# A 128-token product inside a Strassen-ordered MLP: three split products or one plain float32 product

## The chip, the cores and the metric

The kernel runs on one core of a Trainium2 chip. The metric is the device time of one execution in microseconds; the time before is the median of three runs.

## The reference, cut to what matters

One layer of a hybrid backbone is computed for one context sequence of 128 tokens and one latent sequence of 2048 tokens. The change concerns the MLP at the end of the layer, and in it the context tokens alone:

```python
h = rmsnorm(x, norm_ffn_l) * (1.0 + sc2) + sh2
x = x + ga2 * (jnp.square(jax.nn.relu(h @ w_ff1_l)) @ w_ff2_l)
```

D_MODEL is 1024 and D_FF is 4096, all in float32. `h @ w_ff1` of the 128 context tokens is a product of 128x1024 by 1024x4096. The same product of the 2048 latent tokens is sixteen times as large.

## The kernel before, in words

**Tokens.** There are 17 tiles of 128 tokens: tile 0 is the context, tiles 1 to 16 are the latent tokens. The mixer's stages come first; the MLP follows and fills the second half of the span. The first MLP product is the stage in question.

**Split products.** TensorE multiplies `float32r` operands in one product. To keep accuracy, a float32 operand is split by `split4` into a high part (a cast on ScalarE, `wH`) and the remainder (a subtraction on VectorE, `wL`). `mm3` (lines 225 to 227) then issues three products for each 128-deep slice: high x high, high x low, low x high.

**Units.** `w_ff1` is cut into 16 pieces of 256 columns. The latent tokens are two groups of eight tiles, `g` = 0 and 1, so there are 32 units: `n` = 0 to 15 for group 0, 16 to 31 for group 1. In a unit the 2x2 blocks of the weights (column half `i`, contraction half `kh`: the tiles `raw[i, kh]`) are multiplied with the tokens by a Strassen-Winograd scheme of seven products, numbered 1 to 7 and run in `ORDER` = 1, 5, 6, 7, 3, 2, 4. Each product is 4 slices x 3 split products of 512 tokens. The tokens' side lies ready in the tiles `hop[g, o]`, loaded from HBM (`hop_next`, two DMAs of 1 MB each); the weights' side is made in `Unit.weights(o)` from the `raw` tiles, which `Unit.loads` fetches.

**The context tile.** Its 128 tokens do not fit the scheme, so the units of group 1 do it beside the seven products: `Unit.single` multiplies the four blocks of `raw` with the two halves of `x0` (the context tile's activations), and sums them in one PSUM bank, `ps0`, of a block (two units in the first and last block of the group, one unit in the others). Before, `single` uses the split weights that products 1, 2 and 4 need anyway, and one split more (`w[0]`, of `raw[1, 0]`, made for this alone as "product" 0). `x0` is split once by `first_tile`. `single_out` squares the ReLU of the bank and stores it to `z_d[0]`.

**What sets the order.** `seq` lists all (product, unit) pairs. The loop over positions `p` calls, in this order, the loads of position p + LEAD + 8 (14 ahead), the weights of position p + LEAD (6 ahead), the context tile's and the norm's side steps, and the product of position p. Loads and stores all go through SP's DMA queue. The engines' streams are then ordered by a list scheduler that pulls instructions forward when its own plan sees their inputs ready, so that the streams are not simply the order of the code. Tiles named `w` (raw, split and result tiles alike, 49 of 2 KB a partition) share one pool, and the eight PSUM banks named `f` another: a new tile waits until an old one is released.

**The last positions.** From position `last` = len(seq) - 16 on, the loop also prepares the second MLP product (`s_next`, `t_next`: casts and subtractions of `zraw` and `traw`, into `zH`, `zL` and the tokens' tiles).

Of the kernel before, what the change touches and what calls it, by code (L numbers as in the profile page):

```python
# [17 lines left out]
P = 128  # L18
# [34 lines left out]
NV = 7  # L53
LEAD = 6
ORDER = (1, 5, 6, 7, 3, 2, 4)
NK = DFF // P // 2
AHEAD = 3
WINDOWS = [2.46, 0.03, -0.51, 1.06, -1.61, 18.16, 17.58, 18.3,
# [4 lines left out]
def hybrid_step(  # L63
# [7 lines left out]
    V, A, G, T = nc.vector, nc.scalar, nc.gpsimd, nc.tensor  # L71
# [12 lines left out]
    def f32(ap):  # L84
        return ap.bitcast(F32)
# [25 lines left out]
    hop_d = {(g, o): dp.tile([P, 4, 2, 4, P], F32, name=f"hop_{g}_{o}_d") for g in range(2) for o in range(1, 8)}  # L111
    z_d = [dp.tile([4 if a else 1, P, 2, NK, P], F32, name=f"z{a}_d") for a in range(5)]
    s1_d, s2_d = ([dp.tile([4, P, NK, P], F32, name=f"s{i}{g}_d") for g in range(2)] for i in (1, 2))
    t_d = {(i, k): dp.tile([P, 512], F32, name=f"t{i}_{k}_d") for i in (5, 6, 7, 4) for k in range(NK)}

# [96 lines left out]
    def w512(name, dt=F32):  # L212
        return wp.tile([P, 512], dt, tag="w", name=name)
# [7 lines left out]
    def mm3(ps, trip, first=True, last=True, more=False):  # L221

        n = len(trip)
        for i, (lh, ll, rh, rl) in enumerate(trip):
            T.matmul(ps, lh, rh, start=first and i == 0, stop=False, skip_group_check=more)  # L225
            T.matmul(ps, lh, rl, start=False, stop=False, skip_group_check=more)  # L226
            T.matmul(ps, ll, rh, start=False, stop=last and i == n - 1, skip_group_check=more)  # L227
# [47 lines left out]
    with ExitStack() as ph:  # L275
# [8 lines left out]
        def pt():  # L284
            return ppt.tile([P, 512], F32, tag="pt", name="pt", bufs=3)
# [7 lines left out]
        for d in range(2):  # L293
            m = p1.tile([P, P], F32, tag=f"mcum{d}", name=f"mcum{d}", bufs=1)
# [102 lines left out]
        ps = pt()  # L397
# [378 lines left out]
        for bi in range(len(BLOCKS)):  # L776
            nxt = prep_block(bi + 1) if bi + 1 < len(BLOCKS) else None
            if bi == 0:
                order = [(1, 0), (1, 1), (1, 2), (0, 0), (0, 1), (1, 3), (0, 2), (0, 3)]
            else:  # L780
                order = [(gi, h) for gi in (1, 0) for h in range(4)]
            order = order + [(2, h) for h in range(4)]
            at = {e: n for n, e in enumerate(order)}
            tile_of = {}
            for n, (gi, h) in enumerate(order):
                u = us[n] if bi == 0 and n < 3 else feature_tile(blk, bi, gi, h)
# [141 lines left out]
    hops = {}  # L928
    hop_order = [(g, o) for g in range(2) for o in ORDER]
    hop = {}  # L930

    def hop_tile(dt, n):

        side, bufs = ("A", 2) if n else ("B", 5)
        return hops[side].tile([P, 4, 2, 4, P], dt, tag="hop", name="hop", bufs=bufs)

    def hop_next():
        g, o = hop_order.pop(0)
        hop[g, o] = t = hop_tile(F32R, o in ORDER[:2])
        for k in range(0, 4, 2):  # L940
            load(out=f32(t)[:, k : k + 2], in_=hop_d[g, o][:, k : k + 2])


    with ExitStack() as ph:
# [234 lines left out]
        units = [unit(t, 0) for t in range(NT)] + [unit(t, 1) for t in [0] + list(range(NT - 1, 0, -1))]  # L1179
# [205 lines left out]
        for i, u in enumerate(units):  # L1385
            w = p2 if i <= NT else p3
            at(i - 3 if i > PL else -10, u["prep_loads"])
            at(i - 1, u["scan_loads"])
            n = len(u["prep"])
# [5 lines left out]
            if i >= NT:  # L1395
                at(i, lambda u=u: o_loads(u))
                first, second = o_steps(u)
# [66 lines left out]
    def bank():  # L1464
        return psq.tile([P, 512], F32, tag="f", name="f", bufs=8)

    def add(out, a, b, op=ALU.add):
        V.tensor_tensor(out=out, in0=a, in1=b, op=op)  # L1468

    def split4(src, name="w"):  # L1470

        h = wp.tile([P, 4, P], F32R, tag="w", name=name + "H")
        lo = wp.tile([P, 4, P], F32R, tag="w", name=name + "L")
        A.copy(h, src)  # L1474
        add(lo, src, f32(h), ALU.subtract)
        return h, lo

    def as4(t):
        return t.rearrange("p (a d) -> p a d", a=4)


    NP = DFF // 256
    x0 = []

    class Unit:
# [14 lines left out]
        def weights(self, o):  # L1500

            a, w, t = self.raw, self.w, self.t
            if o == 1:
                w[1] = split4(a[0, 0])
            elif o == 5:
                t["s"] = as4(w512("s"))
                add(t["s"], a[1, 0], a[1, 1])
                w[5] = split4(t["s"])
            elif o == 6:
                add(t["s"], t["s"], a[0, 0], ALU.subtract)  # L1510
                w[6] = split4(t["s"])
            elif o == 7:
                d = as4(w512("d"))
                add(d, a[0, 0], a[1, 0], ALU.subtract)
                w[7] = split4(d)
            elif o == 3:
                add(t["s"], a[0, 1], t["s"], ALU.subtract)
                w[3] = split4(t["s"])
            elif o == 2:
                w[2] = split4(a[0, 1])  # L1520
            elif o == 0:
                w[0] = split4(a[1, 0])
            else:
                w[4] = split4(a[1, 1])

# [58 lines left out]

        def single(self, o, ps, i, first, last):

            if o not in (1, 2, 0, 4):
                return
            c = (2 * i + (o in (0, 4))) * P
            k0 = 4 * (o in (2, 4))  # L1590
            h, lo = self.w[o]
            mm3(ps[:, c : c + P], [(h[:, kp, :], lo[:, kp, :], x0[0][k0 // 4][:, kp, :], x0[1][k0 // 4][:, kp, :])
                                   for kp in range(4)], first=first, last=last)

    def single_out(units, ps):
        n = 256 * len(units)
        z = w512("z0")
        A.activation(z[:, :n], ps[:, :n], AF.Relu)
        add(z[:, :n], z[:, :n], z[:, :n], ALU.mult)
        for i, u in enumerate(units):  # L1600
            store(out=z_d[0][0, :, :, u.jp, :], in_=z[:, i * 256 : i * 256 + 256].rearrange("p (a t) -> p a t", a=2))

    def first_load():
        for i in range(2):
            r = as4(w512("x0"))
            load(out=r, in_=h2_d[0][:, i * 4 : i * 4 + 4, :])
            x0.append(r)

    def first_tile():
        pieces = [split4(r, "x0") for r in x0]  # L1610
        x0[:] = [[h for h, _ in pieces], [lo for _, lo in pieces]]


    pairs = [(9 + 2 * i, 10 + 2 * i) for i in range(4)] + [(1 + 2 * i, 2 + 2 * i) for i in range(4)]
# [14 lines left out]
    def moving(i, k):  # L1629

        if (i, k) in t_d:
            return t_d[i, k]
        return rows2(k, *{1: (0, 0), 3: (1, 1), 2: (1, 0)}[i])
# [4 lines left out]
    def fetch(src, name="r2"):  # L1638
        t = w512(name)
        load(out=t, in_=src)  # L1640
        return t
# [142 lines left out]
    def t_ahead(n, upto):  # L1784
        while n < len(products) and len(traws) < min(upto, NK):
            traws.append(fetch(moving(products[n][0], len(traws)), "traw"))

    def t_next(n, k):

        if n < len(products):  # L1790
            t_ahead(n, k + 4)
            tiles[n].append(t_build(traws[k], k))
            if k == NK - 1:
                traws.clear()
# [11 lines left out]
    units = {n: Unit(n) for n in range(2 * NP)}  # L1806
    seq = []
    for b in blocks:
        order = ORDER if b[0] < NP else ORDER[:-1] + (0, 4)
        seq += [(o, n, b) for o in order for n in b]  # L1810
    begun = set()

    def weights_at(p):
        if p < len(seq):
            o, n, _ = seq[p]
            units[n].weights(o)

    def loads_at(p):
        if p < len(seq) and seq[p][1] not in begun:
            begun.add(seq[p][1])  # L1820
            units[seq[p][1]].loads()
# [7 lines left out]
    half = [p for p, e in enumerate(seq) if e[1] == NP][0]  # L1829
    later = []  # L1830
    for j, t in enumerate(range(8, -1, -1)):
        st = h2_steps(t, bank, lambda: w512("junk"), w512)
        p = 10 + 19 * j // 2
        later += [(p + (-4, 0, 1, 2, 4, 5)[k] if k < 6 else p + 2 * k - 6, st[k]) for k in range(len(st))]
    later.sort(key=lambda e: e[0])
    last = len(seq) - 16
    ps0 = None
    for p, (o, n, b) in enumerate(seq):
        u = units[n]
        loads_at(p + LEAD + 8)  # L1840
        weights_at(p + LEAD)
        while later and later[0][0] <= p:
            later.pop(0)[1]()
        if p == half - 20:
            first_load()
        if p == half - 12:
            first_tile()
        if o:
            u.step(o)
        if u.g:  # L1850
            if o == 1 and n == b[0]:
                ps0 = bank()
            u.single(o, ps0, b.index(n), o == 1 and n == b[0], o == 4 and n == b[-1])
            if o == 4 and n == b[-1]:
                single_out([units[m] for m in b], ps0)
        if half - 11 <= p < half + 3 and (half - p) % 2:
            hop_next()
        e = p - last
        if e >= 0 and e % 2:
            if e // 2 == 0:  # L1860
                for m in range(AHEAD):
                    s_next(m, True)
                t_ahead(0, 4)
            elif e // 2 < 5:
                for k in range(4 * (e // 2) - 4, 4 * (e // 2)):
                    t_next(0, k)
                if e // 2 <= AHEAD:
                    s_next(e // 2 - 1, False)
                    s_next(AHEAD + e // 2 - 1, True) if e // 2 < 3 else None
# [4 lines left out]
    for m, (n, i, u, q) in enumerate(todo):  # L1874
# [6 lines left out]
        if q == 0:  # L1881
            ps = bank()
# [4 lines left out]
        h, lo = sops.pop(m)  # L1887
# [7 lines left out]
        if i in (1, 5, 6) and mm < 28:  # L1895
            while pending and mm >= pending[0][0] + 2:
                _, k, r = pending.pop(0)
                sums(i, k, r)
            for k in range(NK):
                if mm == k * 3 // 2:  # L1900
# [57 lines left out]
```

## Time and profile before

| | |
|---|---|
| median of three runs | 2669.81 us (2667.17 to 2671.09) |
| profiled execution: span | 2670.2 us; the page gives no time apart from the span |
| TensorE busy (PE) | 2625.4 us, 98% |
| weight loads (PEld) | 2192.3 us, 82% |
| VectorE (DVE) | 1790.4 us, 67% |
| ScalarE (ACT) | 1245.7 us, 47% |
| DMA | 580.89 MB, mean 218 GB/s |
| granted TensorE clock, mean | 0.994 |
| context tile's products, first and last start | 1599.5 us and 1991.0 us |

PE rows are matmuls, PEld rows the loads of the stationary operand that belong to them. A matmul's duration in the trace runs from its start to its modelled end, and neighbours overlap in it, so the price of one in a stream is the distance of the starts. L225 to L227 are the three lines of `mm3`, wherever it is called; the tile names (`hop`, `x0H`, `zH`) tell the stages apart. L1468 is a helper of VectorE, L1474 the cast of `split4`.

### The profile page before, as it was taken

The numbers are of one execution on the slowest core, as the hardware profiler recorded it, in microseconds if no ns is written. First come the engines' busy times: TensorE is split into PE (matmuls) and PEld (weight loads), VectorE is DVE, ScalarE is ACT, GpSimd is POOL, SyncE is SP. The second block draws the span as 40 slices with busy tenths as digits, with TensorE's granted clock in tenths as the row PEclk, the third lists the DMA queues.
The fourth block names the chain that finished last, engine by engine and source line by source line (L and its number), as shares of the span: only waits on it lengthen the run. The fifth ranks groups of instructions, "written<-read, shape, count | busy, mean of one in ns | idle before, by whom it ended". The sixth has DMA issues, their size and how long they took to land.

```text
span 2670.2 us, 45051 instructions
## 1 busy us (share of the span) xinstructions
PE 2625.4 (98%) x15714; PEld 2192.3 (82%) x15714; DVE 1790.4 (67%) x3694; ACT 1245.7 (47%) x3092; POOL 230.1 (9%) x448
## 2 busy tenths in 40 slices
PE   9999999999999999999999999999999999999998
PEld 5999998787887777788888888888888787888887
DVE  5867655766666778875677885556565556774874
ACT  4755555655555657763455543333242432332441
POOL 3111213111111111110000000000000000000000
PEclk9999999999999999999999999999999999999999
DMA  8967638654445657875877786343369979786782
GB/s 290 295 200 225 185 109 285 199 163 151 154 159 167 211 182 259 293 269 178 288 221 233 251 298 215 108 125 103 109 197 372 328 263 310 263 255 206 234 260 89
DMA packets 499753, 580.89 MB, mean 218 GB/s; under 512 B 35692, under 2 KB 298268, under 8 KB 495942
## 3 DMA queue, kind: packets, MB, share of 16 engines
q1 hardware_dynamic: 499526, 578.03, 67.1%
q8 instruction: 123, 2.02, 0.3%
q14 instruction: 104, 0.85, 0.1%
HBM read 398.14 MB, written 179.74 MB: 216 GB/s over the span
## 4 chain that ended last, share of the span: by engine, by line
PE 86%; DMA 6%; DVE 4%; ACT 2%; issue 1%; POOL 1%; SPq 0%; DVEq 0%; POOLq 0%; ACTq 0%
PE f L227 17%; PE f L225 17%; PE f L226 17%; PE pj L225 7%; PE pj L227 6%; PE pj L226 6%; PE pd L991 3%; PE pm L225 1%; PE pm L227 1%; PE pm L226 1%; DMA raw<-in_w_mod_dram 1%; DMA qT<-qT_d 1%; PE pd L1164 1%; PE pd L1165 1%; PE pt L605 1%
## 5 line engine op out<-in xcount | busy, mean ns | idle before, releaser
L225 PE MATMUL f<-hop,zH 128*128 128x512 f32 x960 | 376.5, 393 | 1.2 <-ACT zH L1474 1.2
L226 PE MATMUL f<-hop,zH 128*128 128x512 f32 x960 | 377.1, 393 | 0.0
L227 PE MATMUL f<-hop,zL 128*128 128x512 f32 x960 | 376.9, 393 | 0.0
L225 PE MATMUL f<-hop,wH 128*128 128x512 f32 x896 | 354.1, 396 | 0.3 <-issue 0.3
L226 PE MATMUL f<-hop,wH 128*128 128x512 f32 x896 | 350.7, 391 | 0.0
L227 PE MATMUL f<-hop,wL 128*128 128x512 f32 x896 | 350.0, 392 | 0.0
L1474 ACT CAST zH<-zraw 128x512 fp32r<-128x512 f32 x240 | 146.8, 620 | 298.8 <-DMA zraw<-s_d 89.2
L225 PEld LDWEIGHTS f<-hop,zH 128*128 128x128 f32 x960 | 180.4, 188 | 43.7 <-ACT zH L1474 1.6
L227 PEld LDWEIGHTS f<-hop,zL 128*128 128x128 f32 x960 | 180.3, 188 | 41.9 <-issue 0.9
L226 PEld LDWEIGHTS f<-hop,zH 128*128 128x128 f32 x960 | 180.2, 188 | 41.8 <-issue 0.9
L1468 DVE TENSOR_TENSOR zL<-zraw,zH 128x512 fp32r<-128x512 f32 x240 | 162.8, 687 | 69.0 <-ACT zH L1474 53.9
L227 PEld LDWEIGHTS f<-hop,wL 128*128 128x128 f32 x896 | 168.3, 188 | 37.6
L226 PEld LDWEIGHTS f<-hop,wH 128*128 128x128 f32 x896 | 168.5, 188 | 35.4
L225 PEld LDWEIGHTS f<-hop,wH 128*128 128x128 f32 x896 | 168.4, 188 | 35.4 <-issue 0.7
L225 PE MATMUL pj<-kH,wH 128*128 128x386 f32 (+2 forms) x568 | 190.5, 338 | 2.0 <-ACT junk L581 1.1
L227 PE MATMUL pj<-kH,wL 128*128 128x386 f32 (+2 forms) x568 | 189.7, 334 | 0.0
L226 PE MATMUL pj<-kL,wH 128*128 128x386 f32 (+2 forms) x568 | 188.9, 334 | 0.0
L182 POOL TENSOR_TENSOR r<-rsq,nhalf 128x1 f32<-128x1 f32 (+1 forms) x38 | 24.1, 633 | 1471.7 <-DVE rsq L181 1471.7
L1468 DVE TENSOR_TENSOR wL<-raw,wH 128x512 fp32r<-128x512 f32 x112 | 76.1, 687 | 76.4 <-ACT wH L1474 75.5
L551 DVE SCALAR_TENSOR_TENSOR cv<-pj,vec,cv 128x384 f32<-128x384 f32 (+2 forms) x164 | 87.0, 539 | 54.8 <-ACT cv L548 53.6
L225 PEld LDWEIGHTS pj<-kH,wH 128*128 128x128 f32 x568 | 107.0, 189 | 7.7 <-issue 4.7
L1474 ACT CAST wH<-s 128x512 fp32r<-128x512 f32 x96 | 59.3, 620 | 105.5 <-DVE s L1468 105.2
(403 smaller groups left out, 6048.3 us busy)
## 6 DMA issues: line engine op xcount, KB each, us to landing
zraw<-z_d SPq DMA_DIRECT2D x212, 256.0 KB
raw<-in_w_ff_dram SPq DMA_DIRECT2D x128, 256.0 KB
hop<-hop_d SPq DMA_DIRECT2D x28, 1024.0 KB
z_d<-c SPq DMA_DIRECT2D x96, 256.0 KB
zraw<-s_d SPq DMA_DIRECT2D x96, 256.0 KB
raw<-in_w_mod_dram SPq DMA_DIRECT2D x80, 256.0 KB
r<-in_w_ff_dram SPq DMA_DIRECT2D x80, 256.0 KB
s_d<-s SPq DMA_DIRECT2D x64, 256.0 KB
```

The costliest lines, as they stand in the source:

```text
L182: G.tensor_tensor(out=out, in0=t[:np_, :n], in1=nhalf[:np_, :n], op=ALU.pow)
L225: T.matmul(ps, lh, rh, start=first and i == 0, stop=False, skip_group_check=more)
L226: T.matmul(ps, lh, rl, start=False, stop=False, skip_group_check=more)
L227: T.matmul(ps, ll, rh, start=False, stop=last and i == n - 1, skip_group_check=more)
L551: V.scalar_tensor_tensor(out=cv[:, o : o + m], in0=ps[:, s + sh : s + sh + m], scalar=convw[:, w, j : j + 1], in1=cv[:, o : o + m], op0=AL ...
L605: T.matmul(ps[:, i * P : (i + 1) * P], kTt[:, i * P : (i + 1) * P], rhs[:, i * P : (i + 1) * P], start=True, stop=True)
L991: T.matmul(p[:, h, :], lhs[:, h, :], rhs[:, h, :], start=True, stop=True)
L1164: T.matmul(p[:, h, :], u["qT"][:, h, :], s[:, h, :], start=True, stop=False)
L1165: T.matmul(p[:, h, :], u["QK"][:, h, :], u["vn"][:, h, :], start=s is None, stop=True)
L1468: V.tensor_tensor(out=out, in0=a, in1=b, op=op)
L1474: A.copy(h, src)
```

## The change

The context tile's products take the raw float32 weight tile and the raw float32 activations in one plain product for each 128-deep slice, in place of the three split ones. The table `SINGLE` ties each block to a position of the unit: the single of a block is now issued where the weights of product 6, 7, 2 or 4 are made, six positions ahead of that product, and no longer behind products 1, 2, "0" and 4. With it go "product" 0, its split, and the split of `x0`. A unit of group 1 has seven positions in `seq` like one of group 0, where it had eight. The accumulation bank is opened with the first of these singles.

```diff
--- before.py
+++ after.py
@@ -53,6 +53,7 @@
 NV = 7
 LEAD = 6
 ORDER = (1, 5, 6, 7, 3, 2, 4)
+SINGLE = {6: (0, 0), 7: (1, 0), 2: (0, 1), 4: (1, 1)}
 NK = DFF // P // 2
 AHEAD = 3
 WINDOWS = [2.46, 0.03, -0.51, 1.06, -1.61, 18.16, 17.58, 18.3,
@@ -1518,8 +1519,6 @@
                 w[3] = split4(t["s"])
             elif o == 2:
                 w[2] = split4(a[0, 1])
-            elif o == 0:
-                w[0] = split4(a[1, 0])
             else:
                 w[4] = split4(a[1, 1])
 
@@ -1584,13 +1583,11 @@
 
         def single(self, o, ps, i, first, last):
 
-            if o not in (1, 2, 0, 4):
-                return
-            c = (2 * i + (o in (0, 4))) * P
-            k0 = 4 * (o in (2, 4))
-            h, lo = self.w[o]
-            mm3(ps[:, c : c + P], [(h[:, kp, :], lo[:, kp, :], x0[0][k0 // 4][:, kp, :], x0[1][k0 // 4][:, kp, :])
-                                   for kp in range(4)], first=first, last=last)
+            m, kh = SINGLE[o]
+            c = (2 * i + m) * P
+            for kp in range(4):
+                T.matmul(ps[:, c : c + P], self.raw[m, kh][:, kp, :], x0[kh][:, kp, :], start=first and kp == 0,
+                         stop=last and kp == 3)
 
     def single_out(units, ps):
         n = 256 * len(units)
@@ -1605,10 +1602,6 @@
             r = as4(w512("x0"))
             load(out=r, in_=h2_d[0][:, i * 4 : i * 4 + 4, :])
             x0.append(r)
-
-    def first_tile():
-        pieces = [split4(r, "x0") for r in x0]
-        x0[:] = [[h for h, _ in pieces], [lo for _, lo in pieces]]
 
 
     pairs = [(9 + 2 * i, 10 + 2 * i) for i in range(4)] + [(1 + 2 * i, 2 + 2 * i) for i in range(4)]
@@ -1806,14 +1799,22 @@
     units = {n: Unit(n) for n in range(2 * NP)}
     seq = []
     for b in blocks:
-        order = ORDER if b[0] < NP else ORDER[:-1] + (0, 4)
-        seq += [(o, n, b) for o in order for n in b]
+        seq += [(o, n, b) for o in ORDER for n in b]
     begun = set()
+
+    bank0 = {}
 
     def weights_at(p):
         if p < len(seq):
-            o, n, _ = seq[p]
+            o, n, b = seq[p]
             units[n].weights(o)
+            if n >= NP and o in SINGLE:
+                first, last = o == 6 and n == b[0], o == 4 and n == b[-1]
+                if first:
+                    bank0[b[0]] = bank()
+                units[n].single(o, bank0[b[0]], b.index(n), first, last)
+                if last:
+                    single_out([units[m] for m in b], bank0[b[0]])
 
     def loads_at(p):
         if p < len(seq) and seq[p][1] not in begun:
@@ -1834,7 +1835,6 @@
         later += [(p + (-4, 0, 1, 2, 4, 5)[k] if k < 6 else p + 2 * k - 6, st[k]) for k in range(len(st))]
     later.sort(key=lambda e: e[0])
     last = len(seq) - 16
-    ps0 = None
     for p, (o, n, b) in enumerate(seq):
         u = units[n]
         loads_at(p + LEAD + 8)
@@ -1843,16 +1843,7 @@
             later.pop(0)[1]()
         if p == half - 20:
             first_load()
-        if p == half - 12:
-            first_tile()
-        if o:
-            u.step(o)
-        if u.g:
-            if o == 1 and n == b[0]:
-                ps0 = bank()
-            u.single(o, ps0, b.index(n), o == 1 and n == b[0], o == 4 and n == b[-1])
-            if o == 4 and n == b[-1]:
-                single_out([units[m] for m in b], ps0)
+        u.step(o)
         if half - 11 <= p < half + 3 and (half - p) % 2:
             hop_next()
         e = p - last
```

**TensorE, a block of one unit of group 1.** Before: the end of product 4 (`f_22667`) and, right behind it, the context tile's product of the same split weights into its own bank (`f_22603`); the three x0 rows come four times over, once for each 128-deep slice.

```order
L226 MATMUL f_22667<-hop_20924,wH_22616 128x512
L227 MATMUL f_22667<-hop_20924,wL_22617 128x512
L225 MATMUL f_22603<-x0H_20580,wH_22616 128x128
L226 MATMUL f_22603<-x0L_20581,wH_22616 128x128
L227 MATMUL f_22603<-x0H_20580,wL_22617 128x128
```

Now: the end of product 2 of such a unit (`f_21961`), then the context tile's product of the block `raw[0, 1]` of a unit that comes later, in four plain products (one row and a row of three), then product 4 (`f_22025`).

```order
L227 MATMUL f_21961<-hop_20855,wH_21917 128x512
L228 MATMUL f_21961<-hop_20855,wL_21918 128x512
L1589 MATMUL f_22020<-x0_20376,raw_21765 128x128 [waits DMAHW1_49]
L1589 MATMUL f_22020<-x0_20376,raw_21765 128x128 x3
L226 MATMUL f_22025<-hop_20916,wH_21949 128x512 [waits Activation_49]
```

Twelve narrow rows have become four, they read `x0` and `raw` as the DMA left them, and the first of them waits for that DMA where the split ones waited for nothing of their own.

**TensorE, the place of the first of them.** Before: the end of product 7 of unit 14 (`f_20665`) and the start of product 7 of unit 15 (`f_20688`), both still in group 0, 94 rows ahead of the first x0 row of the old order.

```order
L226 MATMUL f_20665<-hop_17707,wH_20523 128x512
L227 MATMUL f_20665<-hop_17707,wL_20524 128x512
L225 MATMUL f_20688<-hop_17707,wH_20552 128x512 [waits Activation_49]
L226 MATMUL f_20688<-hop_17707,wH_20552 128x512
L227 MATMUL f_20688<-hop_17707,wL_20553 128x512 [waits DVE_49]
```

Now: the same two products with the first plain product of unit 16 (`raw_20513`) between two rows of the second.

```order
L227 MATMUL f_20657<-hop_17707,wH_20523 128x512
L228 MATMUL f_20657<-hop_17707,wL_20524 128x512
L226 MATMUL f_20680<-hop_17707,wH_20552 128x512 [waits Activation_49]
L227 MATMUL f_20680<-hop_17707,wH_20552 128x512
L1589 MATMUL f_20809<-x0_20374,raw_20513 128x128 [waits DMAHW7_49,DMAHW4_49,DVE_49]
L228 MATMUL f_20680<-hop_17707,wL_20553 128x512 [waits DVE_49]
```

The scheduler pulled one product forward alone; the other three of its block stand 58 rows further on. It waits for two DMAs, the raw tile's and x0's, and for a VectorE instruction that releases the PSUM bank: the addition that reads product 6 of unit 15.

**SP, one unit's turn in the middle of group 1.** Before: a unit's last stores (`z1_d` of product 4, `z0_d` of the context tile) and behind them the four loads of a later unit's raw tiles.

```order
L1534 DMA z1_d_99<-c11_21864 128x4x128 [waits DMAHW4_49,Activation_49]
L1537 DMA s21_d_106<-s2_21868 128x4x128 [waits DMAHW5_49,DVE_49]
L1534 DMA z1_d_99<-c21_21916 128x4x128 [waits DMAHW6_49,DVE_49]
L1601 DMA z0_d_98<-z0_21932 256x1x128 [waits DMAHW7_49,DVE_49]
L1498 DMA raw_21987<-in_w_ff1_dram 128x4x128 [waits DMAHW0_49,PE_49]
L1498 DMA raw_21989<-in_w_ff1_dram 128x4x128 [waits DMAHW1_49,PE_49]
L1498 DMA raw_21991<-in_w_ff1_dram 128x4x128 [waits DMAHW2_49]
L1498 DMA raw_21993<-in_w_ff1_dram 128x4x128 [waits DMAHW3_49]
```

Now: the same stretch.

```order
L1533 DMA z1_d_99<-c11_21550 128x4x128 [waits DMAHW2_49,Activation_49]
L1536 DMA s21_d_106<-s2_21554 128x4x128 [waits DMAHW3_49,DVE_49]
L1499 DMA raw_21581<-in_w_ff1_dram 128x4x128 [waits DMAHW4_49,PE_49]
L1499 DMA raw_21583<-in_w_ff1_dram 128x4x128 [waits DMAHW5_49,PE_49]
L1499 DMA raw_21585<-in_w_ff1_dram 128x4x128 [waits DMAHW6_49,PE_49]
L1499 DMA raw_21587<-in_w_ff1_dram 128x4x128 [waits DMAHW7_49]
L1533 DMA z1_d_99<-c21_21577 128x4x128 [waits DMAHW0_49,DVE_49]
L1598 DMA z0_d_98<-z0_21597 256x1x128 [waits DMAHW1_49,DVE_49]
```

The four loads stand ahead of the last two stores now, and three of the four wait for TensorE where two did. One of the three waits for a plain product, which was the last to read an earlier unit's raw tile; before, the raw tiles were last read by ScalarE and VectorE.

## The prediction

> **What bounds the kernel now.** The engines' row of the page comes first: TensorE is busy 98% of the span, no other engine over 67%. Then the stretches (columns: us, busy time of PE, PEld, DVE, ACT and POOL with counts, granted clock, DMA share, GB/s): the first row is the group 0 part of the first MLP product, the second holds the context tile's products, the third is the start of the second MLP product.
>
> ```profile
> PE 2625.4 (98%) x15714; PEld 2192.3 (82%) x15714; DVE 1790.4 (67%) x3694; ACT 1245.7 (47%) x3092; POOL 230.1 (9%) x448
> ```
>
> ```profile
> 1290.00:1600.00 310.00, 309.67 (x1389) 253.67 (x1388) 243.79 (x412) 155.81 (x325) 5.65 (x9) 1.00 0.81 261
> 1600.00:1991.00 391.00, 391.00 (x2097) 335.19 (x2096) 236.79 (x373) 127.05 (x233) 0.00 (x0) 1.00 0.48 141
> 1991.00:2250.00 259.00, 257.81 (x1112) 207.54 (x1112) 145.10 (x223) 82.49 (x143) 0.00 (x0) 1.00 0.91 319
> ```
>
> From 1600 to 1991 us TensorE never stops (391.00 of 391.00), at full clock, while VectorE is busy 236.8 us, ScalarE 127.1 us and the DMA engines 0.48. So in this stage the end is set by the sum of the start-to-start distances on TensorE. A microsecond taken from that sum is a microsecond of the kernel, as long as the engines beside it still feed it; a microsecond taken from the others is none. The groups of that stretch, by form, give the counts:
>
> ```profile
> L225 PE MATMUL f<-hop,wH 128*128 128x512 f32 x444 | 176.4, 398 | 0.0
> ...
> L227 PE MATMUL f<-x0H,wL 128*128 128x128 f32 x255 | 70.2, 275 | 0.0
> L226 PE MATMUL f<-x0L,wH 128*128 128x128 f32 x255 | 70.1, 275 | 0.0
> L225 PE MATMUL f<-x0H,wH 128*128 128x128 f32 x255 | 67.5, 265 | 0.0
> ```
>
> The durations overlap, so the price has to come from starts. The timeline of TensorE around one context product (start, duration) shows it:
>
> ```profile
> 1603.43 0.39 PE L227 MATMUL f<-hop,wL 128*128 128x512 f32 x1
> 1603.66 0.22 PE L225 MATMUL f<-x0H,wH 128*128 128x128 f32 x1
> ...
> 1604.83 0.28 PE L227 MATMUL f<-x0H,wL 128*128 128x128 f32 x1
> 1604.94 0.45 PE L225 MATMUL f<-hop,wH 128*128 128x512 f32 x1
> 1605.23 0.39 PE L226 MATMUL f<-hop,wH 128*128 128x512 f32 x1
> ```
>
> A wide product moves the next start by 0.23 us (1603.43 to 1603.66). The twelve narrow ones and one wide take 1603.66 to 1605.23, 1.57 us; less the wide one's 0.23 that is 1.34 us, 0.112 us for each narrow product. A quarter of the columns costs half the time.
>
> **The change part by part. The products removed.** 16 units x 4 blocks x 12 = 768 narrow split products, at 0.1117 us (1.34/12): 85.8 us. The whole stretch agrees: 3 x 444 = 1332 wide products at 0.23 are 306.4 us, and 391.0 less that leaves 84.6 us for the 765 narrow ones, 0.1106 each.
>
> **The products added.** 16 x 4 x 4 = 256 plain float32 products of 128 columns. The trace has plain products of this very form, raw float32 on both sides, in the mixer: L1248, four for each of 17 tiles, 68 in the program.
>
> ```profile
> L1248 PE MATMUL pm<-vg,wsT x104: 270/275/356, 521.1 to 863.2; 128*128 128x128 f32 x104
> ...
> L1248 PE MATMUL pj<-vg,wsT x32: 271/275/377, 483.1 to 919.8; 128*128 128x128 f32 x32
> ```
>
> ```profile
> 521.07 1.05 PE L1248 MATMUL pm<-vg,wsT 128*128 128x128 f32 x8
> 521.88 0.47 PE L225 MATMUL pm<-wH,hH 128*128 128x512 f32 x1
> 522.20 0.39 PE L226 MATMUL pm<-wL,hH 128*128 128x512 f32 x1
> ```
>
> 104 + 32 = 136 records are two for each product. Their price in a stream of wide split products, as here: 521.07 to 522.20 less 0.23 is 0.90 us for eight records, 0.1125 each, what a narrow split product costs. So a plain product costs 0.225 us against 0.335 us for three split ones, and the change between the kinds costs nothing that these rows show. 256 x 0.225 = 57.6 us.
>
> That two records do the work of a full float32 product for the price of two narrow split ones needs a reason. Plain products of 512 columns (line 332, at the start of the mixer) give it:
>
> ```profile
> 12.40 4.45 PE L332 MATMUL pj<-raw,scond 128*2 128x512 f32 x10
> 16.78 0.40 PE L341 MATMUL pm<-ident,first 2*128 2x2 f32 x4
> ```
>
> Ten records in 4.38 us are 0.438 us each, 1.9 times the wide split product's 0.23. So a plain record does cost about twice by its columns; for 128 columns a quarter of 0.438 is 0.110, just under the 0.112 at which narrow products follow each other anyhow. The doubled cost lies under a floor that the split products pay too.
>
> Here a rule of the Trainium skill speaks against the change: FP8 and Floating Point Precision, "TensorE Precision Notes", says that true FP32 takes four passes through the array, where three split products are three. By it, four times the narrow price, the sum would be 256 x 4 x 0.1117 = 114.4 us and the kernel slower; the trace agrees with four passes' worth of columns (two records of double length), and its 128-column rows show that they cost two.
>
> **ScalarE and VectorE.** 16 splits of `raw[1, 0]` and two of `x0` go: 18 casts and 18 subtractions.
>
> ```profile
> L1474 ACT CAST wH<-raw 128x512 fp32r<-128x512 f32 x62 | 37.9, 619 | 0.0
> ...
> L1468 DVE TENSOR_TENSOR wL<-raw,wH 128x512 fp32r<-128x512 f32 x62 | 42.5, 689 | 72.5 <-ACT wH L1474 71.6
> ```
>
> 18 x 0.62 = 11 us of ScalarE and 18 x 0.69 = 12 us of VectorE, both beside a full TensorE: nothing on the path. They make room for the shorter stage: VectorE's 237 - 12 = 225 us stand against 391 - 28 = 363 us. That the engines can feed group 1 at this pace is shown by the 1290 to 1600 row, where the same seven products follow each other without the context tile: TensorE 309.67 of 310 with VectorE at 79%, DMA at 0.81.
>
> **The singles moved.** They are issued six positions earlier. The first one now stands between two products of unit 15. In the old trace that place is 94 wide products before the first x0 row at 1599.5: 94 x 0.23 = 21.6, about 1577.9 us. Whatever it waits for stops TensorE, since the products behind it wait in line, and through them the copies out of PSUM. It waits for three things:
>
> ```profile
> L225 PE MATMUL f<-x0H,wH x256: 220/274/277, 1599.5 to 1990.8; 128*128 128x128 f32 x128
> ```
>
> ```profile
> 1566.82 2.75 SPq L1498 DMA_DIRECT2D raw<-in_w_ff_dram  x1
> ...
> 1575.54 0.42 SPq L1498 DMA_DIRECT2D raw<-in_w_ff_dram  x1
> ```
>
> ```profile
> 1570.84 1.14 ACT L1474 CAST x0H<-x 128x512 fp32r<-128x512 f32 x2
> ...
> 1581.07 0.62 ACT L1474 CAST wH<-raw 128x512 fp32r<-128x512 f32 x1
> 1583.98 0.62 ACT L1474 CAST wH<-raw 128x512 fp32r<-128x512 f32 x1 [2.28 <-DMA raw<-in_w_ff_dram]
> ```
>
> ```profile
> 1575.15 0.69 DVE L1468 TENSOR_TENSOR x<-f,x 128x512 f32<-128x512 f32 x1 [0.76 <-PE f L227]
> ```
>
> x0 was there at 1570.8, when its cast ran. The bank's last reader, the addition of unit 15's product 6, ended at 1575.15 + 0.69 = 1575.8. The raw tile of unit 16 was issued at 1566.8; its first cast was at 1581.07, so it landed by then. Unit 17's, issued at 1575.54, ended a wait at 1583.98: 8.4 us. The same 8.4 us from 1566.8 (or from the issue's end, 1569.6) give 1575.2 to 1578.0. The wait is 0 to 3.2 us (1581.1 less 1577.9), once; I take 0, since the row that measures a landing gives 0.1 us at most. Later singles read tiles that products of their own unit have used, or will use within 14 positions.
>
> **Loads and the tail.** On SP the four raw loads of a unit move ahead of the last two stores, and wait for TensorE three times instead of twice. Behind them stand stores, which nobody on TensorE waits for in this stage; the loads run two units ahead of their use, and a unit takes 84 x 0.23 + 16 x 0.225 = 22.9 us. With seven positions a unit, the last 16 positions begin two products earlier before the end, and the preparation of the second MLP product with them. The first wait of that stage in the third row is part of 259.00 - 257.81 = 1.2 us: 0 to 1.2 us gained, I take 0.
>
> **The sum.** 85.8 - 57.6 = 28.2 us. The profiled span is 2670.2 us, 0.4 over the median of the runs, and the page shows no other time of that execution, so I take the sum from the median: 2669.8 - 28.2 = **2641.6 us**. The bounds of the terms: 84.6 x 768/765 - 57.6 = 27.3 us at the least for the products, 256 x (0.335 - 2 x 0.110) = 29.4 us if a plain record gets down to a quarter of the 512-column one; 3.2 us lost at the first single, 1.2 us gained at the tail; the runs' own spread of 2 us each way. That is 2637 to 2648.
>
> **The rivals.** *Four passes, paid one by one.* If the plain products of this stage cost four narrow prices, the 256 cost 114.4 us, 28.6 more than the 768: 2698.4 us. It decides from 85.8/256 = 0.335 us for a plain product on, three records' worth. Against it stand the two records of 0.1125 us at L1248; for it, only that those have other operands in other banks. 5%.
>
> *Holes in the feeding.* The raw tiles now live until TensorE has read them, the loads wait for it, and SP is one queue. If each of 16 units lost 1 us on a late tile, the time would be 2657.6; at 28.2/16 = 1.8 us a unit the gain would be gone. For it: the third wait on SP, and the DMA share of 0.81 just before (the 1290 to 1600 row), where the `hop` tiles of group 1 begin to come. Against it: DMA at 0.48 in the stage, and two units of lead. 6%.
>
> *The gain is given back in the second MLP product.* Its first 259 us run with DMA at 0.91 and TensorE at 257.81.
>
> ```profile
> 2000.00:2100.00 100.00, 98.81 (x427) 79.74 (x426) 57.25 (x88) 36.01 (x64) 0.00 (x0) 1.00 0.99 356
> ```
>
> In the first 100 us the share is 0.99, and TensorE still has 98.81. If earlier traffic had drained its queue in the 28 us that now are gone, half the gain would come back as waits: 2655.7 us. Against it: the loads are issued by positions, which move along with TensorE. 5%.
>
> *The change doesn't do what it says:* a plain product might run as one record; then 256 x 0.112 = 28.7 us are left, and the time is 2612.7. Against it, the same two records. 1%.
>
> **How the numbers follow.** The forecast has 83%. Its own range, 2637 to 2648, is widened to 2636 to 2656, which takes in the case of half the gain given back and part of the holes; left out are four passes, the single record, the deeper holes and some of the forecast's own tails, together under 2 in 10. A measurement of this kernel can tell 0.2%, 5.3 us, from no change. Faster by more: forecast, half given back, most of the holes and the single record, 0.93. Within it: holes of about 1.8 us a unit, 0.02. Slower: four passes, 0.05.
>
> **What would show it.** After, the plain products must appear as 512 records of 128x128 at about 0.112 us apart, and the stretch from the first of them to the start of the second MLP product must have TensorE busy throughout. The old 1600 to 1991 stretch must be about 28 us shorter, and the second MLP product as long as before. Wrong would be: 1024 records, or records 0.2 us apart (four passes); idle time of TensorE put down to the DMA of `raw` (holes); idle time at `zH` after the boundary (given back); a stop of over 3 us at the first plain product.

## The result and the profile after

The changed kernel takes 2641.31 us (median of four runs, 2636.78 to 2643.67); the kernel before, measured beside it, 2668.49 us (2665.95 to 2671.09). The ratio is 0.9896, with a 95% interval of 0.9884 to 0.9908: faster by 27 us by the medians, by 25 to 31 us by the interval.

The page of after first, its row of engines:

```profile
PE 2592.2 (98%) x15458; PEld 2161.4 (82%) x15458; DVE 1778.8 (68%) x3676; ACT 1236.1 (47%) x3074; POOL 229.8 (9%) x448
```

TensorE has 256 records fewer (15714 less 15458), which is 768 less 512, and VectorE and ScalarE have 18 instructions fewer each. TensorE's share of the span is the same 98%.

Two rows of each kernel cut the program into stages: the listing of single instruction forms by line, with count, shortest/median/longest duration in ns, and the start of the first and of the last in us. The first `wL` record opens the first MLP product, and the first `zL` record the second. Before:

```profile
L227 PE MATMUL f<-hop,zL x960: 387/389/500, 1991.6 to 2661.0; 128*128 128x512 f32 x192
...
L227 PE MATMUL f<-hop,wL x896: 387/389/402, 1279.9 to 1989.6; 128*128 128x512 f32 x180
```

After (the same `mm3` stands one line lower), with the row of the plain products:

```profile
L228 PE MATMUL f<-hop,zL x960: 387/389/500, 1956.4 to 2625.8; 128*128 128x512 f32 x192
...
L228 PE MATMUL f<-hop,wL x896: 387/389/476, 1273.8 to 1955.7; 128*128 128x512 f32 x180
...
L1589 PE MATMUL f<-x,raw x512: 270/275/275, 1571.5 to 1936.7; 128*128 128x128 f32 x171
```

From the first `wL` to the first `zL` it is 1991.6 - 1279.9 = 711.7 us before and 1956.4 - 1273.8 = 682.6 us after: 29.1 us less. From the first to the last `zL` it is 669.4 us in both. The two spans differ by 35.3 us (2670.2 and 2634.9); the other 6.1 us lie ahead of the first MLP product, in code that the change does not touch. In the experiments below, where that code is the same too, the stage begins anywhere from 1270.8 to 1281.1 us, so a part that does not change varies by 10 us from one execution to the next. A part of this goes with the granted clock, which in both profiles falls below full only ahead of this stage: in the stretches 400 to 500, 600 to 700 and 900 to 1000 us it is 0.91, 0.98 and 0.97 before, 0.95, 0.98 and 0.98 after. That is some 3 to 5 of the 6.1 us, as an estimate from these rounded shares. Over all the runs it is not the whole, since the profiles of e2 and e4 (below) both show 0.91 in the first of these stretches and full clock in the others, and their stages begin at 1270.8 and 1275.9 us. For that reason the comparisons of profiles below go by the length of the stage, and the times of the kernels by medians.

The stretches of after (us, busy time of PE, PEld, DVE, ACT and POOL with counts, granted clock, DMA share, GB/s): the whole first MLP product, the part with the context tile, and the second MLP product to the end of the span.

```profile
1273.40:1955.90 682.50, 682.50 (x3273) 569.03 (x3272) 475.11 (x772) 278.76 (x549) 5.65 (x9) 1.00 0.65 204
...
1571.50:1955.90 384.40, 384.40 (x1939) 324.91 (x1938) 246.88 (x387) 128.20 (x234) 0.00 (x0) 1.00 0.54 165
...
1955.90:2634.90 679.00, 669.08 (x2889) 540.78 (x2887) 426.66 (x695) 226.72 (x417) 10.78 (x17) 1.00 0.76 258
```

The same last stretch before:

```profile
1991.10:2670.20 679.10, 669.12 (x2890) 540.85 (x2889) 427.87 (x695) 228.86 (x420) 11.74 (x17) 1.00 0.77 258
```

TensorE has no hole in the first MLP product of after (682.50 of 682.50), at full clock, with VectorE and the DMA engines far from full. In the second its busy time is 669.1 us in both kernels. So the stage is shorter by what TensorE no longer issues, and nothing of that is lost behind it.

The price of a plain record, from TensorE's timeline (start, duration) of after around one context product:

```profile
1604.75 0.39 PE L228 MATMUL f<-hop,wL 128*128 128x512 f32 x1
1604.98 1.05 PE L1589 MATMUL f<-x,raw 128*128 128x128 f32 x8
1605.79 0.47 PE L226 MATMUL f<-hop,wH 128*128 128x512 f32 x1
1606.10 0.39 PE L227 MATMUL f<-hop,wH 128*128 128x512 f32 x1
```

From 1604.98 to 1606.10 are 1.12 us; less the wide product's 0.23 us, eight records cost 0.89 us, 0.111 each. A narrow split record cost 0.1117.

### The profile page after: what moved, and what is told of

It is laid out like the page before. It is cut to its first block, busy times and chain, and to the rows that moved or that the text cites. A ratio compares the mean times of both kernels' runs of the same rounds, so it can differ in the third digit from the quotient of the medians.

```text
span 2634.9 us, 44534 instructions
## 1 busy us (share of the span) xinstructions
PE 2592.2 (98%) x15458; PEld 2161.4 (82%) x15458; DVE 1778.8 (68%) x3676; ACT 1236.1 (47%) x3074; POOL 229.8 (9%) x448
## 4 chain that ended last, share of the span: by engine, by line
PE 86%; DMA 5%; DVE 5%; ACT 1%; issue 1%; SPq 1%; POOL 1%; DVEq 0%; POOLq 0%; ACTq 0%
PE f L227 16%; PE f L228 16%; PE f L226 16%; PE pj L226 7%; PE pj L228 6%; PE pj L227 6%; PE pd L992 3%; PE f L1589 2%; PE pm L226 1%; PE pm L227 1%; PE pm L228 1%; PE pt L606 1%; DMA raw<-in_w_mod_dram 1%; PE pd L1165 1%; PE pd L1166 1%
## 5 line engine op out<-in xcount | busy, mean ns | idle before, releaser
L552 DVE SCALAR_TENSOR_TENSOR cv<-pj,vec,cv 128x384 f32<-128x384 f32 (+2 forms) x164 | 87.0, 539 | 54.1 <-ACT cv L549 52.8
L227 PEld LDWEIGHTS pj<-kL,wH 128*128 128x128 f32 x568 | 107.4, 189 | 0.5
```

Source lines behind the costliest of these rows:

```text
L552: V.scalar_tensor_tensor(out=cv[:, o : o + m], in0=ps[:, s + sh : s + sh + m], scalar=convw[:, w, j : j + 1], in1=cv[:, o : o + m], op0=AL ...
```

## The experiments

Two theories stood against each other at the start. By the first, the gain is the difference of TensorE records alone, 768 against 512, each at the same 0.11 us for 128 columns. By the second, a part of it comes from what else the change did: 18 splits fewer on ScalarE and VectorE, the products issued six positions earlier, the loads moved on SP. A second pair of theories concerns the price itself: a plain record costs no more than a split one because both wait for something that does not depend on the columns, or because plain products are no dearer by the column.

Each experiment is measured beside the kernel before, which took 2668.71 us with the first four and, on another chip, 2668.57 us with the last three. All stage lengths, read as above, and the counts of context records:

| kernel | context records | stage, us | median, us | ratio to before (95%) |
|---|---|---|---|---|
| before | 768 split, 128 columns | 711.7 | 2668.49 | |
| after | 512 plain, 128 columns | 682.6 | 2641.31 | 0.9896 (0.9884 to 0.9908) |
| e1: plain, in the old place | 512 plain, 128 | 681.9 | 2639.04 | 0.9893 (0.9880 to 0.9907) |
| e2: split, without the extra split | 768 split, 128 | 712.4 | 2668.39 | 1.0002 (0.9992 to 1.0011) |
| e3: plain, each product twice | 1024 plain, 128 | 740.3 | 2694.10 | 1.0100 (1.0086 to 1.0114) |
| e4: high parts only | 256 split, 128 | 654.8 | 2612.59 | 0.9792 (0.9779 to 0.9805) |
| e5: plain, 256 columns | 512 plain, 256 | 736.1 | 2691.33 | 1.0084 (1.0069 to 1.0099) |
| e6: split, 256 columns | 768 split, 256 | 716.6 | 2672.95 | 1.0014 (1.0005 to 1.0024) |
| e7: plain, 64 columns | 512 plain, 64 | 683.9 | 2641.07 | 0.9898 (0.9881 to 0.9914) |

### e1: the plain products alone, in the old place and with all the splits

Against before, in `single` (and `x0raw[:] = x0` ahead of the split in `first_tile`):

```diff
-            h, lo = self.w[o]
-            mm3(ps[:, c : c + P], [...], first=first, last=last)
+            r = self.raw[int(o in (0, 4)), k0 // 4]
+            for kp in range(4):
+                T.matmul(ps[:, c : c + P], r[:, kp, :], x0raw[k0 // 4][:, kp, :], start=first and kp == 0,
+                         stop=last and kp == 3)
```

> The kernel before with one thing of the change: the context tile's products are plain float32 products of the raw tiles, at their old places behind products 1, 2, 0 and 4. The split of raw[1, 0], the split of x0 and the eighth position of a unit stay, though nothing reads those splits. Theory (TensorE's sum of narrow records, 0.112 us each, 768 become 512): the whole gain is here, 28 us, about 2640 us. Rival 1 (the gain is the work taken from ScalarE and VectorE): that work is still there, so about 2668 us. Rival 2 (the gain is the new order, the earlier issue and the shorter sequence): also about 2668 us.

It took 2639.04 us. The two rows of its stages:

```profile
L227 PE MATMUL f<-hop,zL x960: 387/389/500, 1963.0 to 2632.9; 128*128 128x512 f32 x192
...
L227 PE MATMUL f<-hop,wL x896: 387/389/403, 1281.1 to 1961.4; 128*128 128x512 f32 x180
```

The stage is 1963.0 - 1281.1 = 681.9 us, against 682.6 in after. With the splits still made and the products, loads and splits in their old order, the whole gain is there. The other parts of the change are worth nothing that these runs can tell.

### e2: the extra split alone taken out

Against before. Product 0's weights are those of product 1, so the context tile's block is multiplied with the wrong weights; the instructions are otherwise the same.

```diff
-                w[0] = split4(a[1, 0])
+                w[0] = w[1]
```

> The kernel before without the 16 splits of raw[1, 0]: the context product of that block uses the split of raw[0, 0] instead, so that block's sum is of other weights. All 768 narrow split products stay, at their places. Theory: ScalarE and VectorE lose 16 x 0.62 = 10 us and 16 x 0.69 = 11 us that lay beside a full TensorE, so no change: 2668.5 us within 0.2%. Rival 1 (splits on the path): up to 10 us less, about 2658 us.

It took 2668.39 us, ratio 1.0002. The row of the group of the weights' subtractions on VectorE (count, busy time and mean of one, idle time ahead of them) and, of the listing, the stage rows:

```profile
L1468 DVE TENSOR_TENSOR wL<-raw,wH 128x512 fp32r<-128x512 f32 x96 | 65.1, 686 | 84.4 <-ACT wH L1474 80.9 <-DMA raw<-in_w_ff_dram 3.4
```

```profile
L227 PE MATMUL f<-hop,zL x960: 387/390/504, 1983.2 to 2652.6; 128*128 128x512 f32 x192
...
L227 PE MATMUL f<-hop,wL x896: 387/390/402, 1270.8 to 1981.1; 128*128 128x512 f32 x180
```

In e1's group of the same name there are 112 subtractions, here 96. Sixteen splits, 11 us of VectorE, are gone, and the stage is 712.4 us against 711.7. Work taken from an engine beside a full TensorE is worth nothing here.

### e3: every plain product twice

Against after. The context tile's sums come out doubled.

```diff
-            for kp in range(4):
-                T.matmul(ps[:, c : c + P], self.raw[m, kh][:, kp, :], x0[kh][:, kp, :], start=first and kp == 0,
-                         stop=last and kp == 3)
+            for kp in range(8):
+                T.matmul(ps[:, c : c + P], self.raw[m, kh][:, kp // 2, :], x0[kh][:, kp // 2, :],
+                         start=first and kp == 0, stop=last and kp == 7)
```

> The changed kernel with each of its 256 plain products issued twice, so the context tile's first product comes out doubled. 1024 records in place of 512. Theory (each record 0.112 us on the path): 57 us more than the changed kernel's 2641, 2698 us, which is also what four paid passes would have given. Rivals 1 and 2 (the gain lies in splits or order, narrow records are hidden or cheap): clearly less than 2698, between 2641 and 2670 us.

It took 2694.10 us. Its stage rows:

```profile
L228 PE MATMUL f<-hop,zL x960: 386/390/500, 2018.5 to 2687.9; 128*128 128x512 f32 x192
...
L228 PE MATMUL f<-hop,wL x896: 386/390/477, 1278.2 to 2017.8; 128*128 128x512 f32 x180
```

The stage is 740.3 us, 57.7 more than in after for 512 records more, 0.113 each. By the medians it is 52.8 us more than after (55.1 more than e1, which was measured beside it), by the interval of e3 50 to 58 us (2691.6 to 2699.1 less 2641.3). The price of the added products in the sum, 57.6 us for 256, lies in that interval, near its upper end.

### e4: the high parts only, one product for three

Against before. The low parts of the weights and of the activations are left out of the context tile's product, so a part of that product is missing.

```diff
-            h, lo = self.w[o]
-            mm3(ps[:, c : c + P], [...], first=first, last=last)
+            h = self.w[o][0]
+            for kp in range(4):
+                T.matmul(ps[:, c : c + P], h[:, kp, :], x0[0][k0 // 4][:, kp, :], start=first and kp == 0,
+                         stop=last and kp == 3)
```

> The kernel before with one split product (high x high) in place of three in the context tile's products, which leaves out the low parts there. 256 narrow records in place of 768, all splits and places as before. Theory (0.1117 us a record whatever its kind): 512 x 0.1117 = 57 us less than before, about 2611 us. Rivals 1 and 2: no change, about 2668 us.

It took 2612.59 us. Stage rows and, in a second fence, TensorE's timeline around one context product:

```profile
L227 PE MATMUL f<-hop,zL x960: 387/390/506, 1930.7 to 2600.1; 128*128 128x512 f32 x192
...
L227 PE MATMUL f<-hop,wL x896: 387/390/447, 1275.9 to 1929.7; 128*128 128x512 f32 x180
```

```profile
1701.07 0.56 PE L1593 MATMUL f<-x0H,wH 128*128 128x128 f32 x4
1701.46 0.45 PE L225 MATMUL f<-hop,wH 128*128 128x512 f32 x1
1701.74 0.40 PE L226 MATMUL f<-hop,wH 128*128 128x512 f32 x1
```

Four records cost 1701.74 - 1701.07 - 0.23 = 0.44 us, 0.110 each. With 256, 512, 768 and 1024 records of 128 columns (e4, after, before, e3) the stage is 654.8, 682.6, 711.7 and 740.3 us: steps of 27.8, 29.1 and 28.6 us for 256 records, whether those are split or plain ones. The count of records is what the stage follows. This version is faster than both kernels, but only by what it leaves out.

### e5 and e6: the same products with 256 columns

e5 is against after, e6 against before. Each context product writes 256 columns, the whole of its unit's part of the bank, so that the products of the two column halves of a unit land on each other there. The 256 columns come from two neighbouring slices of the activations, of which one does not belong to the product. The count of records is unchanged. The first diff is e5's, the second e6's.

```diff
+            c = 2 * i * P
...
+                j = 2 * (kp // 2)
+                T.matmul(ps[:, c : c + 2 * P], self.raw[m, kh][:, kp, :], x0[kh][:, j : j + 2, :],
+                         start=first and kp == 0, stop=last and kp == 3)
```

```diff
+            c = 2 * i * P
...
+            j = [0, 0, 2, 2]
+            mm3(ps[:, c : c + 2 * P], [(h[:, kp, :], lo[:, kp, :], x0[0][k0 // 4][:, j[kp] : j[kp] + 2, :],
+                                        x0[1][k0 // 4][:, j[kp] : j[kp] + 2, :]) for kp in range(4)],
+                first=first, last=last)
```

> The changed kernel with each plain product 256 columns wide in place of 128: the moving side takes two neighbouring slices of x0, and the two column halves of a unit share one region of the bank, so the context tile's first product is another sum. 512 records as before. Theory (a plain record costs the larger of the 0.112 us at which narrow records follow each other and its columns, a 512-column one 0.438 us): 256 columns cost 0.219 us, 512 x (0.219 - 0.112) = 55 us more than 2641, about 2696 us. Rival (a narrow record costs 0.112 us whatever its width, because of its weight load alone): 2641 us.

> The kernel before with each narrow split product 256 columns wide in place of 128, in the same manner (another sum in the context tile's first product). 768 records as before. Theory (a split record costs the larger of 0.112 us and its columns, a 512-column one 0.23 us): 256 columns cost 0.115 us, 768 x (0.115 - 0.112) = 2 to 3 us more than 2668.5, about 2671 us; so that at this width the split kernel is the faster one by 25 us, and the change would have lost. Rival (the narrow records are paced by their columns): 0.115 + 0.055 us or twice 0.112, 40 to 85 us more.

e5 took 2691.33 us, e6 2672.95 us. e5's stage rows, and TensorE's timeline around one of its products:

```profile
L228 PE MATMUL f<-hop,zL x960: 387/390/500, 2013.2 to 2682.6; 128*128 128x512 f32 x192
...
L228 PE MATMUL f<-hop,wL x896: 387/390/586, 1277.1 to 2012.5; 128*128 128x512 f32 x180
```

```profile
1703.37 0.39 PE L228 MATMUL f<-hop,wL 128*128 128x512 f32 x1
1703.59 1.89 PE L1591 MATMUL f<-x,raw 128*128 128x256 f32 x8
1705.13 0.59 PE L226 MATMUL f<-hop,wH 128*128 128x512 f32 x1
1705.55 0.40 PE L227 MATMUL f<-hop,wH 128*128 128x512 f32 x1
```

e6's stage rows, and the first two and the last of 18 narrow products in its timeline:

```profile
L227 PE MATMUL f<-hop,zL x960: 387/389/500, 1992.2 to 2661.6; 128*128 128x512 f32 x192
...
L227 PE MATMUL f<-hop,wL x896: 387/389/403, 1275.6 to 1990.1; 128*128 128x512 f32 x180
```

```profile
1709.88 0.28 PE L225 MATMUL f<-x0H,wH 128*128 128x256 f32 x1
1709.99 0.28 PE L226 MATMUL f<-x0L,wH 128*128 128x256 f32 x1
...
1711.91 0.28 PE L227 MATMUL f<-x0H,wL 128*128 128x256 f32 x1
```

A plain record of 256 columns costs (1705.55 - 1703.59 - 0.23)/8 = 0.216 us, half of what one of 512 columns costs in the prediction's rows (0.43 to 0.44 us) and nearly twice the 0.111 us of 128. By the stage, e5 pays 53.5 us more than after for 512 records (736.1 - 682.6), which gives the same price. The expected 2696 us was 5 us too high, of which the 0.219 us expected for a record accounts for 1.5. A split one costs (1711.91 - 1709.99)/16 = 0.120 us; it had cost 0.112 with half the columns. So plain records do pay by their columns, and split ones hardly pay for 256. With 256 columns the order is turned round: plain loses to split by 18 us (2691.33 against 2672.95).

### e7: plain products with 64 columns

Against after. The first and the third of the four slices multiply the left 64 of the 128 columns, the second and the fourth the right 64, so half of the sum is left out. The count of records is unchanged.

```diff
+                j = 64 * (kp % 2)
+                T.matmul(ps[:, c + j : c + j + 64], self.raw[m, kh][:, kp, :], x0[kh][:, kp, j : j + 64],
+                         start=first and kp == 0, stop=last and kp == 3)
```

> The changed kernel with each plain product 64 columns wide in place of 128: even slices fill the left half of a region, odd slices the right one, so half of the context tile's first product is left out. 512 records as before. At 128 columns the plain record's columns (a quarter of 0.438, 0.110 us) and the pace of narrow records (0.112 us) are too close to be told apart. Theory (the pace of narrow records is that of their weight loads): 64 columns cost 0.112 us as well, 2641 us. Rival (the plain record is paced by its columns): 0.055 us, 512 x 0.057 = 29 us less, about 2612 us.

It took 2641.07 us, as after did. Stage rows, and the timeline around one product:

```profile
L228 PE MATMUL f<-hop,zL x960: 387/389/500, 1957.0 to 2626.4; 128*128 128x512 f32 x192
...
L228 PE MATMUL f<-hop,wL x896: 387/392/476, 1273.1 to 1956.3; 128*128 128x512 f32 x180
```

```profile
1703.26 1.00 PE L1590 MATMUL f<-x,raw 128*128 128x64 f32 x8
1704.07 0.48 PE L226 MATMUL f<-hop,wH 128*128 128x512 f32 x1
1704.38 0.39 PE L227 MATMUL f<-hop,wH 128*128 128x512 f32 x1
```

Eight records cost 1704.38 - 1703.26 - 0.23 = 0.89 us, 0.111 each, the price of 128 columns. Halving the columns brings nothing, so at 128 the columns are not what a plain record pays for. What does not change is that each record loads a 128x128 block of weights (15458 loads and 15458 products on the page of after). No run varied the loaded block alone, but the mixer has other blocks. Of before, rows of weight loads (count, busy time and mean ns of one, idle time ahead of them), and a stretch of float16 products with 64 columns:

```profile
L1073 PEld LDWEIGHTS <-X 128*128 128x128 f16 x680 | 33.7, 98 | 39.6 <-issue 28.0 <-DVE P L1065 8.8 <-ACT gw L1197 0.3
...
L1248 PEld LDWEIGHTS pm<-vg,wsT 128*128 128x128 f32 x104 | 13.5, 191 | 0.9
...
L332 PEld LDWEIGHTS pj<-raw,scond 128*2 128x2 f32 x32 | 2.6, 84 | 9.7 <-issue 8.6 <-DMA xh<-in_x_sample_dram 0.7 <-DMA x<-in_x_prompt_dram 0.3
```

```profile
522.79 0.28 PE L1073 MATMUL pd<-P,X 128*128 128x64 f16 x4
522.91 0.28 PE L1075 MATMUL pd<-X,P 128*128 128x64 f16 x4
```

Float16 records with a 128x128 block each follow each other at 0.12/4 = 0.03 us, so the floor of 0.111 us is no price that every record pays. And a float32 load of 128 columns lasts 107 ns longer than one of 2 (191 less 84), a float16 load 14 ns (98 less 84). A floor set by the pace of the float32 loads fits all these rows, but the float16 products have another moving side as well: the load is the likely name of the floor, and not shown alone.

## Why the prediction was right

**What bounds.** A full TensorE from the first context product on: after has 384.40 of 384.40 us there. Holds.

**Products removed, products added.** Forecast were 85.8 us for 768 and 57.6 us for 256 products of two records. The plain products are 512 records, as forecast, at 0.111 us where 0.1125 stood (the mixer's rows were 1% high), and the split ones at (711.7 - 654.8)/512 = 0.111 where 0.1117 stood. The gain is 27.2 us by the medians and 29.1 us by the stage; 28.2 us was forecast, and the bounds of 27.3 to 29.4 hold the stage's; the medians' lies just below them. The forecast of the time, 2641.6 us, came within 0.3 us partly by luck: it was taken from 2669.8 us, where the kernel before took 2668.49 beside the changed one, and the gain by the medians was 1.0 us smaller than forecast, so the two differences nearly cancel.

**The reason for the price.** The prediction let the doubled column cost lie just under the floor of narrow products: 0.110 under 0.112. e5 and e7 show both parts: 0.216 us at 256 columns, 0.111 at 64. The 0.438 us behind the 0.110 was a little high: the ten records were priced up to the start of another kind of product behind them, while the last of the ten starts at 16.26 us, so that nine distances make 3.86 us, 0.429 each. A quarter of that is 0.107 us, and the half of e5's 0.216 is 0.108. The floor lies above the columns' cost by 0.003 to 0.004 us at 128 columns. The Trainium skill's rule (FP8 and Floating Point Precision, "TensorE Precision Notes") says that true FP32 takes four passes. The trace has two records, and e5 agrees with four passes' worth of columns, two of double length. But at 128 columns they cost two narrow records, not four: the rival's 2698.4 us would need 0.447 us a product (114.4/256), no gain at all 0.335, and about 0.222 was measured. The rival is refuted for this width; at 256 columns the change would have lost time.

**ScalarE and VectorE.** Put at nothing. With the splits kept the gain is whole (e1), and with 16 of the 18 gone and nothing else changed there is none (e2).

**The singles moved.** The first was put 298.0 us into the stage (1577.9 less 1279.9), with a wait of 0 to 3.2 us, taken as 0. TensorE's timeline of after at that place:

```profile
1571.27 0.39 PE L227 MATMUL f<-hop,wH 128*128 128x512 f32 x1
...
1571.50 0.38 PE L1589 MATMUL f<-x,raw 128*128 128x128 f32 x2
```

It starts at 1571.50, which is 297.7 us after 1273.8, and 0.23 us after the wide product ahead of it: no wait. The value taken was the right one.

**Loads and the tail.** Put at nothing, of up to 1.2 us. The stretch of the second product is 679.00 us after and 679.10 before: nothing.

**The rivals.** Holes in the feeding would stand as idle time of TensorE in the first MLP product, of which there is none. Given back later would stand as a longer second product, and that is the same to 0.1 us. The single record would be 256 plain records; there are 512. Such a gain does exist, but only for a product that leaves its low parts out (e4, 2612.59 us).

**What was not sized.** The profiled execution of after is 35.3 us shorter than that of before, of which the first MLP product accounts for 29.1. Read span against span, the forecast would have seemed 7 us too small. The 6.1 us between lie in the unchanged mixer; its granted clock accounts for a part of them, and what else makes its length vary by 10 us stays open.

## What to carry to other kernels

Where TensorE is full, count its records and price each at the larger of a floor (here 0.111 us with 128x128 float32 weights) and its columns' cost (here 0.23 us for 512 columns of a split product, 0.43 us for a plain one); the durations of narrow records, 0.27 us, overlap and say nothing of it. A plain float32 product is two records of double column cost and a split one three of single cost, so plain wins while the product is narrow and loses when it is wide: 27 us won at 128 columns, 18 us lost at 256. An estimate puts the crossing at about 205 columns (3 x 0.115 us, between the split record's 0.111 at 128 and 0.120 at 256, against 2 x 0.216 us x N/256). The splits that the plain form saves were worth nothing here, beside a full TensorE; no run shows a case in which the engines that make them are late.

## What the runs showed of the hardware that was not expected

Split products of 256 columns follow each other at 0.120 us, where 128 columns take 0.111: twice the columns in this product would have cost only 4 us more (e6, 2672.95 against 2668.57). The expectation had been 0.115 us, half of the wide product's 0.23. The profile of before could have told: in its mixer, split products of 258 columns start 0.121 us apart (385.77 to 387.58 us, 15 distances), and ones of 386 columns 0.175 (385.42 to 385.77 us, two distances). With 0.23 at 512 these lie near a line of 0.43 us for each thousand columns and about 0.01 us for each record, an estimate from these three widths. Where that 0.01 us goes, no run shows.
